# Second block's attention heads: score products alternate between the array's row halves, value products between its column halves

## The chip, the cores and the metric

One core of a Trainium2 chip runs the whole program in one launch. The metric is the device time in microseconds of one execution. The profile is of one further execution, with times relative to the start of its span.

## What is computed

The reference runs two transformer blocks of two layers each over 256 tokens of width 1024, in float32. The change lies in the second block's mixer alone. Each of its two layers projects the normed input to queries, keys and values of heads of width 64, and has three kinds of heads:

```python
def fox_attention(q, k, v, log_f):              # 4 "forget" heads, causal
    s = q k^T / 8 + c_q - c_k                   # c: running sum of the forget gates
def dilated_attention(q, k, v):                 # 4 heads, three dilations, merged by their log sums
def nsa_attention(q, kc, vc, ks, vs, kw, vw, gates, ...):
    # 8 heads in 2 key groups of 4; three branches, mixed by gates:
    # compressed keys; selected blocks (with 4 blocks and top 16, every block); a window of 512 (all keys)
    o = gb[..., 0:1] * o_c + gb[..., 1:2] * o_s + gb[..., 2:3] * o_w
```

Every branch is softmax(scores) times values. The mixer's outputs are projected back by `w_out`, normed and added to the input, and a feed-forward part follows.

## The kernel before, in words

The kernel is written with tile pools, and a planner turns the program into one fixed instruction order for each engine: it goes through the program in order of emission, simulates the time, and issues on each engine the earliest emitted instruction whose inputs and slots are there. Semaphores are set by it.

The 256 tokens are two token tiles of 128. Large products (`mm3`, L220 to L222) take three products of float32r parts each. They write to PSUM tiles `g`, of which there are four, one bank each. Another four banks, `t`, serve transposes and value products.

`attend` (L711) holds the mixer's heads. Projections of column groups 5, 1, 2, 0, 3, 4 (`proj`) stand between them. `heads` (L739) transposes queries and keys, so that head features lie on partitions: an even head, or key group 0, on partitions 0 to 63, an odd head, or key group 1, on 64 to 127. A score product then contracts over 64 partitions and uses half of the array's rows. Queries and keys are float32, so that one product in the code is two passes (two weight loads and two matmuls) in the trace.

- `heads4` (L619) makes a token tile's four dilated ('d') or forget ('f') heads. For each parity of the head a `g` tile gets the mask by a product with an identity (L629, L631), then two score products (L634), all on one row half. Forget heads also get two products of depth 4 with the row of forget sums (L639). A softmax follows (L513: maximum on VectorE, scaling by -1/8 on GpSimd, one exponential per head on ScalarE, reciprocal and scaling on VectorE).
- `nsa_scores` (L654) does the same for one key group `g`, one token tile `t` and one branch `w` (selected or window). At token tile 0 one `g` tile holds all four heads; at token tile 1 two `g` tiles hold two heads each, with 256 keys. L661 is the mask product, L663 the score products.
- The second half of each of these generators transposes the probabilities (L535) and, in `heads4`, multiplies them with the values (L649). Value products have 64 output features, so each uses half of the array's columns.
- `nsa_out` (L694) sums the three branches of both key groups in one `t` tile: group 0 in partitions 0 to 63, group 1 in 64 to 127 (L706).
- `units` (L759) starts each generator, keeps it in a queue, and runs the oldest one's second half when the queue is longer than `DEPTH` = 6.

After `attend`, `wide` (L453) makes the output projection in four `g` tiles. Its first half needs the dilated and forget heads alone.

Of the kernel before, what the change touches and what calls it, by code (L numbers as in the profile page):

```python
# [9 lines left out]
F32 = mybir.dt.float32  # L10
# [19 lines left out]
# which tags of a pool share slots, and the slots' counts  # L30
# [23 lines left out]
class Layout:  # L54
    """Weights as a sequence of [128, 2048] tiles, with the place of each by name."""
# [4 lines left out]
    def add(self, name, w, nk, ncol):  # L60
        """w [K, N] in tiles of nk row blocks by ncol columns; name -> [column group][row group]"""
# [39 lines left out]
def lay_second(inp, l):  # L101
    """The second block's weights and vectors of layer l"""
# [22 lines left out]
def causal_masks():  # L125
    """What the scores of four heads (token tile 0) or two (1) are added to"""
# [6 lines left out]
def constants():  # L133
    """Constants of the shapes alone, each [128, n] float32"""
# [28 lines left out]
DEPTH = 6  # L163


class Core:
# [4 lines left out]
    def tile(self, pool, shape, dt=F32, tag=None, bufs=None):  # L171
        """A tile of a pool: tags of one size share slots, as SHARE has it; BUFS has the slots' counts"""
# [20 lines left out]
    def slot(self):  # L193
        """The pool of the next tile of weights: one in 4 in self.more, if there is any"""
# [3 lines left out]
    def weights(self, src, nk, ncol, pool=None, tag=None, cols=1024):  # L198
        """A tile of weights, nk row blocks by ncol columns: each block as two float32r parts whose sum it is"""
# [17 lines left out]
    def mm3(self, ps, a, b, first, last):  # L217
        """ps += (a0 + a1)^T (b0 + b1) without a1^T b1, which is below float32's last place"""
# [22 lines left out]
    def gemm_t_steps(self, pss, X, tiles, banks=True, tail=1):  # L241
        """The same, step by step: a tile, or of the last ones a token tile"""
# [28 lines left out]
    def rsqrt(self, v, eps, fam, n=1, scale=1.0):  # L271
        """(scale * v + eps) ** -0.5 for a [128, n] tile"""
# [8 lines left out]
    def stats(self, chunks, fam):  # L281
        """mean and variance over the chunks (at most 512 columns each) -> [128, 2]"""
# [10 lines left out]
    def pair(self):  # L293
        """A [128, 8, 256] operand's two parts"""
# [8 lines left out]
    def split(self, shape, src, tag, scale=None, pool=None):  # L303
        """(scale * src) as two float32r parts; src may be in PSUM"""
# [15 lines left out]
class Second(Core):  # L320
    """One layer of the second block, in place on the two token tiles X"""
# [30 lines left out]
    def consts2(self, cm):  # L352
        """Constants of the second block in the types its products take"""
# [10 lines left out]
    def rms_hT(self, X, g, apart=False):  # L364
        """rms_norm(X) * g, transposed: two float32r parts [128, 8, 256]"""
# [1417 lines left out]
```

## Time and profile before

| | us |
|---|---|
| timed runs | 2775.9, 2768.64, 2766.63 |
| median | 2768.64 |
| span of the profiled execution | 2762.7 |
| TensorE busy | 2662.2 (96%) |
| VectorE busy | 1952.3 (71%) |
| ScalarE busy | 1381.0 (50%) |
| 16 DMA engines | 48.6% for weights and rows |

The span runs from the first instruction to the last; the timed runs include what lies around it. Busy times are from the page's first part. The heads of the second block lie at 2058 to 2192 us (first layer) and 2434 to 2553 us (second layer).

### The profile page before, as it was taken

Reading aid. Unit: us, or ns where it says so; the run is one execution under the profiler, and the core shown is the slowest. Engines: PE = TensorE matmul, PEld = TensorE weight load, DVE = VectorE, ACT = ScalarE, POOL = GpSimd, SP = SyncE. Lnnn points to the kernel's source line nnn. Section 1 sums busy time; section 2 is a strip of 40 time slices with the busy share of each in tenths; the row PEclk is TensorE's granted clock in tenths of the full one; section 3 lists DMA queues with packets and bytes.
Section 4 is the critical chain, followed back from the end, with each engine's and each line's share of the span. In section 5 each row is a group of like instructions: output and inputs, shape, how many; then the busy total and the mean of one; then the engine's idle time right before and its main releaser. Section 6 shows DMA issues by size and latency. Waiting matters only on the chain.

```text
span 2762.7 us, 44974 instructions
## 1 busy us (share of the span) xinstructions
PE 2662.2 (96%) x17024; PEld 2276.8 (82%) x17024; DVE 1952.3 (71%) x3898; ACT 1381.0 (50%) x2522; POOL 177.2 (6%) x411
## 2 busy tenths in 40 slices
PE   7999999999999999999999999989989999999999
PEld 5977999977989888887797897979866699776897
DVE  4888977888867633355688997766665589556795
ACT  3555565545555422234754654544554366544563
POOL 0010111000100100001100110010010000000000
PEclk9999999999999999999999999999988799999999
DMA  7566556565536522232555433645644256542454
GB/s 252 185 223 206 169 174 217 171 206 175 171 115 204 170 92 92 94 97 94 170 161 204 150 128 99 201 157 190 191 152 154 70 168 197 169 162 87 152 194 157
DMA packets 127915, 443.31 MB, mean 160 GB/s; under 512 B 14889, under 2 KB 19113, under 8 KB 127697
## 3 DMA queue, kind: packets, MB, share of 16 engines
q1 hardware_dynamic: 127696, 440.43, 48.6%
q8 instruction: 134, 2.20, 0.3%
q14 instruction: 85, 0.69, 0.1%
HBM read 435.09 MB, written 5.28 MB: 159 GB/s over the span
## 4 chain that ended last, share of the span: by engine, by line
PE 47%; DVE 2%; ACT 1%; POOL 1%; issue 1%; DMA 0%; DVEq 0%; POOLq 0%; SPq 0%; ACTq 0%
PE g L221 11%; PE g L220 11%; PE g L222 11%; PE g L663 1%; PE t L221 1%; PE t L222 1%; PE t L220 1%; PE t L535 1%; PE t L706 1%; PE t L1269 1%; PE t L1103 1%; PE t L1140 0%; PE t L1166 0%; PE t L1253 0%; DMA raw<-in_w_dram 0%
## 5 line engine op out<-in xcount | busy, mean ns | idle before, releaser
L213 DVE TENSOR_TENSOR lo<-raw,hi 128x512 fp32r<-128x512 f32 (+2 forms) x1280 | 825.8, 685 | 350.8 <-issue 159.5
L210 ACT CAST hi<-raw 128x1024 fp32r<-128x1024 f32 (+2 forms) x644 | 672.3, 1046 | 726.2 <-PE g L221 249.2
L220 PE MATMUL g<-b,hi 128*128 128x256 f32 (+1 forms) x2912 | 829.8, 287 | 2.2 <-ACT hi L210 1.4
L221 PE MATMUL g<-b,hi 128*128 128x256 f32 (+1 forms) x2912 | 827.5, 286 | 3.2 <-DVE b L314 3.2
L222 PE MATMUL g<-b,lo 128*128 128x256 f32 (+1 forms) x2912 | 821.2, 287 | 2.4 <-DVE lo L213 2.3
L221 PEld LDWEIGHTS g<-b,hi 128*128 128x128 f32 x2912 | 547.4, 188 | 12.9 <-DVE b L314 4.9
L220 PEld LDWEIGHTS g<-b,hi 128*128 128x128 f32 x2912 | 546.9, 188 | 13.5 <-ACT b L313 2.5
L222 PEld LDWEIGHTS g<-b,lo 128*128 128x128 f32 x2912 | 540.6, 188 | 11.9 <-DVE lo L213 3.7
L1281 DVE SCALAR_TENSOR_TENSOR yc<-yc,vec,yc 128x256 f32<-128x256 f32 x720 | 346.3, 481 | 10.8
L221 PE MATMUL g<-lo,b 128*128 128x512 f32 (+2 forms) x712 | 274.8, 386 | 2.9 <-DVE lo L213 2.6
L222 PE MATMUL g<-hi,b 128*128 128x512 f32 (+2 forms) x712 | 266.1, 374 | 0.9 <-DVE b L317 0.8
L220 PE MATMUL g<-hi,b 128*128 128x512 f32 (+2 forms) x712 | 256.2, 378 | 9.5 <-ACT h L522 4.4
L220 PEld LDWEIGHTS g<-hi,b 128*128 128x128 f32 x712 | 135.7, 193 | 38.1 <-ACT h L522 6.8
L221 PEld LDWEIGHTS g<-lo,b 128*128 128x128 f32 x712 | 137.0, 192 | 32.0 <-DVE lo L213 8.4
L222 PEld LDWEIGHTS g<-hi,b 128*128 128x128 f32 x712 | 136.9, 192 | 22.4 <-DVE b L317 1.5
L220 PE MATMUL t<-b,hi 128*128 128x256 f32 (+1 forms) x336 | 111.8, 333 | 0.0
L221 PE MATMUL t<-b,hi 128*128 128x256 f32 (+1 forms) x336 | 111.8, 333 | 0.0
L222 PE MATMUL t<-b,lo 128*128 128x256 f32 (+1 forms) x336 | 111.7, 332 | 0.0
L917 PE MATMUL g<-raw,cs 128*32 128x512 f32 x384 | 84.2, 647 | 14.6 <-DMA raw<-in_w_dram 14.5
L480 DVE SCALAR_TENSOR_TENSOR s<-g,vec,s 128x255 f32<-128x255 f32 (+1 forms) x176 | 84.2, 479 | 6.3 <-ACT s L478 4.1
L220 PEld LDWEIGHTS t<-b,hi 128*128 128x128 f32 x336 | 63.0, 187 | 7.5
L222 PEld LDWEIGHTS t<-b,lo 128*128 128x128 f32 x336 | 63.0, 187 | 7.4
(426 smaller groups left out, 3994.7 us busy)
## 6 DMA issues: line engine op xcount, KB each, us to landing
raw<-in_w_dram SPq DMA_DIRECT2D x772, 512.0 KB
b<-in_row_dram SPq DMA_DIRECT2D x16, 512.0 KB
b<-in_ctx_dram SPq DMA_DIRECT2D x4, 512.0 KB
ends<-st SPq DMA_DIRECT2D x8, 256.0 KB
st<-ends SPq DMA_DIRECT2D x8, 256.0 KB
b<-in_x_dram SPq DMA_DIRECT2D x4, 512.0 KB
b<-ctx SPq DMA_DIRECT2D x4, 512.0 KB
raw<-in_w_dram SPq DMA_DIRECT2D x4, 426.0 KB
```

Of the source, the lines that this page charges most:

```text
L210: self.nc.scalar.copy(hi[:, :m], p)
L213: self.nc.vector.tensor_sub(lo[:, q], p[:, q], hi[:, q].bitcast(F32))
L220: t.matmul(ps, a[0], b[0], start=first, stop=False)
L221: t.matmul(ps, a[0], b[1], start=False, stop=False)
L222: t.matmul(ps, a[1], b[0], start=False, stop=last)
L480: nc.vector.scalar_tensor_tensor(c[:, m, j:], ps[:, m, :256 - j], cw[:, ft, 2 - j:3 - j], c[:, m, j:], op0=ALU.mult, op1=ALU.add)
L535: nc.tensor.transpose(ps[:, i * 128:i * 128 + 128], b, self.ident)
L663: nc.tensor.matmul(ps[:, b], qk['nq', a * per + b][s, t * 128:t * 128 + 128], qk[kn, 0][s, :nk], start=False, stop=b == per - 1)
L706: nc.tensor.matmul(po[s].rearrange("p j q -> p (j q)"), pr[kt][:, col:col + 64], PT_[t, w, g, kt], start=False, stop=w == 1 and kt == t, t ...
L917: nc.tensor.matmul(ps[32 * q:32 * q + 32], self.cs[:, h * 4 + q], raw[:, q % 2 * 512:q % 2 * 512 + 512], start=h == 0, stop=h == 1, tile_p ...
L1103: nc.tensor.matmul(p[:, h], kw[:, d, h * 128:h * 128 + 128], vg[:, h * 256:h * 256 + 256], start=True, stop=True)
L1281: e.scalar_tensor_tensor(o, y[:, j:j + 256], w[:, j:j + 1], o, op0=ALU.mult, op1=ALU.add)
```

## The change

The score products of two PSUM tiles, one for each row half, are now issued in turn. `nsa_scores` makes both key groups in one unit: two mask products, then for each head a product of group 0 and one of group 1, then both softmaxes. In `heads4` the products with the forget sums stand right behind the mask, ahead of the scores. Value products alternate between the column halves from one product to the next. The queue of units is four long instead of six, and the list of units at the end has two score units instead of four. The diff also empties comment lines and docstrings, which are not shown.

```diff
-DEPTH = 6
+DEPTH = 4
...
     def heads4(self, kind, base, t, pr, qk, crow, hi, lo):
-        PS = []
-        for par in range(2):
-            ps = self.tile(self.PG, [128, 512], F32, 'g')[:, :2 * nk].rearrange("p (h k) -> p h k", h=2)
+        pss = [self.tile(self.PG, [128, 512], F32, 'g')[:, :2 * nk].rearrange("p (h k) -> p h k", h=2) for _ in range(2)]
+        for par, ps in enumerate(pss):
             flat = ps.rearrange("p h k -> p (h k)")
             if kind == 'f':
                 cm = self.cmb[t] if t == 1 else self.cmb[0][:, :256]
                 nc.tensor.matmul(flat, self.identb, cm, start=True, stop=False)
+                for b in range(2):
+                    h = 2 * b + par
+                    nc.tensor.matmul(ps[:, b], self.c('self')[:4, h * 128:h * 128 + 128], crow[:, :nk], start=False, stop=False)
             else:
                 nc.tensor.matmul(flat, self.ident, self.c(f'dm{t}'), start=True, stop=False)
-            s = slice(64 * par, 64 * par + 64)
-            for b in range(2):
+        for b in range(2):
+            for par, ps in enumerate(pss):
+                s = slice(64 * par, 64 * par + 64)
                 nc.tensor.matmul(ps[:, b], qk[kind + 'q', b][s, t * 128:t * 128 + 128], qk[kind + 'k', b][s, :nk],
-                                 start=False, stop=kind == 'd' and b == 1)
-            if kind == 'f':
...
-            PS.append(self.softmax(ps, 2, nk))
+                                 start=False, stop=b == 1)
+        PS = [self.softmax(ps, 2, nk) for ps in pss]
...
-        for h in range(4):
-            s = slice(64 * (h % 2), 64 * (h % 2) + 64)
+        for b in range(2):
             for kt in range(t + 1):
...
+                for h in (2 * b, 2 * b + 1):
+                    s = slice(64 * (h % 2), 64 * (h % 2) + 64)
...
-    def nsa_scores(self, t, w, kn, gi, g, pr, qk, ga, PT_):
+    def nsa_scores(self, t, w, kn, gi, pr, qk, ga, PT_):
...
-            ps = self.tile(self.PG, [128, 512], F32, 'g').rearrange("p (h k) -> p h k", h=per)
-            nc.tensor.matmul(ps.rearrange("p h k -> p (h k)"), self.identb, self.cmb[t], start=True, stop=False)
+            pss = [self.tile(self.PG, [128, 512], F32, 'g').rearrange("p (h k) -> p h k", h=per) for _ in range(2)]
+            for ps in pss:
+                nc.tensor.matmul(ps.rearrange("p h k -> p (h k)"), self.identb, self.cmb[t], start=True, stop=False)
             for b in range(per):
-                nc.tensor.matmul(ps[:, b], qk['nq', a * per + b][s, t * 128:t * 128 + 128], qk[kn, 0][s, :nk],
-                                 start=False, stop=b == per - 1)
+                for g, ps in enumerate(pss):
+                    s = slice(64 * g, 64 * g + 64)
+                    nc.tensor.matmul(ps[:, b], qk['nq', a * per + b][s, t * 128:t * 128 + 128], qk[kn, 0][s, :nk],
+                                     start=False, stop=b == per - 1)
...
     def nsa_out(self, t, pr, cmp, PT_, hi, lo):
-        for g in range(2):
-            s = slice(64 * g, 64 * g + 64)
-            for w, vn in enumerate(('vs', 'vw')):
-                for kt in range(t + 1):
-                    col = P2[vn] + 64 * g
+        for w, vn in enumerate(('vs', 'vw')):
+            for kt in range(t + 1):
+                for g in range(2):
+                    s, col = slice(64 * g, 64 * g + 64), P2[vn] + 64 * g
...
-        units(scores(0, 0, 0), scores(0, 0, 1))
+        units(scores(0, 0))
...
-        units(scores(0, 1, 0), scores(0, 1, 1))
+        units(scores(0, 1))
...
-        units(four('f', 2, 0), scores(1, 0, 0))
+        units(four('f', 2, 0))
         next(cv, None)
-        units(four('f', 2, 1), scores(1, 0, 1), self.nsa_compressed(0, qk, cmp, ga, PT_), scores(1, 1, 0),
-              self.nsa_out(0, pr, cmp, PT_, hi, lo), self.nsa_compressed(1, qk, cmp, ga, PT_), scores(1, 1, 1),
+        units(four('f', 2, 1), scores(1, 0), self.nsa_compressed(0, qk, cmp, ga, PT_),
+              self.nsa_out(0, pr, cmp, PT_, hi, lo), scores(1, 1), self.nsa_compressed(1, qk, cmp, ga, PT_),
               self.nsa_out(1, pr, cmp, PT_, hi, lo))
```

## Rows read from the trace of the kernel before

**Rows 1.** The page's first part: engine, busy us, share, instructions.
```profile
PE 2662.2 (96%) x17024; PEld 2276.8 (82%) x17024; DVE 1952.3 (71%) x3898; ACT 1381.0 (50%) x2522; POOL 177.2 (6%) x411
...
```

**Rows 2.** Busy time in the stretches around the heads; columns in the first line.
```profile
core 0: us, PE busy (x) PEld busy (x) DVE busy (x) ACT busy (x) POOL busy (x), PEclk, DMA share, GB/s
2092.90:2100.60 7.70, 7.49 (x72) 5.28 (x71) 3.26 (x11) 5.38 (x20) 0.69 (x3) 1.00 0.48 153
2115.60:2161.80 46.20, 46.20 (x193) 30.11 (x192) 26.48 (x87) 16.90 (x54) 5.09 (x11) 0.61 0.20 70
...
2488.50:2524.30 35.80, 35.80 (x192) 24.17 (x191) 22.77 (x75) 15.31 (x49) 3.71 (x9) 0.81 0.28 89
2524.30:2552.90 28.60, 28.09 (x156) 18.58 (x155) 18.42 (x43) 13.35 (x31) 1.27 (x3) 1.00 0.23 73
```

**Rows 3.** The same view, cut where the granted clock changes.
```profile
2119.05:2129.28 10.23, 10.23 (x45) 6.13 (x47) 5.43 (x19) 2.69 (x10) 1.24 (x3) 0.50 0.01 2
...
2136.12:2166.80 30.68, 30.68 (x101) 21.59 (x100) 15.61 (x56) 8.22 (x29) 2.75 (x6) 0.50 0.12 39
...
2504.80:2518.40 13.60, 13.60 (x56) 10.07 (x55) 6.67 (x23) 3.82 (x12) 1.14 (x2) 0.50 0.29 95
```

**Rows 4.** Timeline of TensorE, token tile 0; start us, us, instruction, shapes, count.
```profile
2093.01 1.71 PE L663 MATMUL g<-h,h 64*128 64x128 f32 x16
...
2096.95 0.39 PE L661 MATMUL g<-cmb,identb 128*128 128x512 bf16 x1
2097.27 1.16 PE L663 MATMUL g<-h,h 64*128 64x128 f32 x8
2098.36 0.39 PE L661 MATMUL g<-cmb,identb 128*128 128x512 bf16 x1
...
2099.76 0.63 PE L581 MATMUL t<-cst,s 128*128 128x32 f32 x4
```

**Rows 5.** Timeline of ScalarE after token tile 0's scores.
```profile
2101.33 1.05 ACT L210 CAST hi<-raw 128x1024 fp32r<-128x1024 f32 x1 [0.74 <-DMA raw<-in_w_dram]
```

**Rows 6.** Timeline of TensorE, forget heads of token tile 1, first layer.
```profile
2133.45 1.13 PE L634 MATMUL g<-h,h 64*128 64x256 f32 x4
2134.51 1.13 PE L639 MATMUL g<-s,cst 4*128 4x256 f32 x4
```

**Rows 7.** Timeline of TensorE, scores of token tile 1 in both layers.
```profile
2156.65 0.63 PE L661 MATMUL g<-cmb,identb 128*128 128x512 bf16 x1
...
2159.22 0.61 PE L661 MATMUL g<-cmb,identb 128*128 128x512 bf16 x1
...
2521.56 0.38 PE L661 MATMUL g<-cmb,identb 128*128 128x512 bf16 x1
2521.87 1.13 PE L663 MATMUL g<-h,h 64*128 64x256 f32 x4
2522.93 0.39 PE L661 MATMUL g<-cmb,identb 128*128 128x512 bf16 x1
```

**Rows 8.** Timeline of TensorE, value products of both token tiles, first layer.
```profile
2181.97 1.94 PE L706 MATMUL t<-h,proj 128*64 128x512 f32 x8
2183.85 0.33 PE L535 MATMUL t<-cst,s 128*128 128x128 f32 x1
...
2186.11 4.56 PE L706 MATMUL t<-h,proj 128*64 128x512 f32 x14
2190.60 0.49 PE L220 MATMUL g<-h,b 128*128 128x512 f32 x1
2191.03 1.07 PE L706 MATMUL t<-h,proj 128*64 128x512 f32 x2
2192.03 0.49 PE L221 MATMUL g<-h,b 128*128 128x512 f32 x1
```

**Rows 9.** Softmax groups by line, both layers; a wait of TensorE, first layer.
```profile
L517 DVE TENSOR_REDUCE s_a<-g 128x2 f32<-128x512 f32 x24 | 16.2, 675 | 1.6 <-PE g L639 1.6
...
L518 POOL TENSOR_SCALAR s_a<-s_a 128x2 f32<-128x2 f32 x32 | 13.7, 429 | 202.8 <-DVE s_a L517 150.6 <-DVE s_a L526 36.0 <-DVE gx L586 7.1
...
L522 ACT ACTIVATE h<-g,s_a 128x256 f32<-128x256 f32 x48 | 22.3, 472 | 27.8 <-POOL s_a L518 27.8
...
PE g L220 <- ACT h L522: 2.0, 1, 2.0
```

More of the change, by code (lines that the diff above doesn't have):

```diff
@@ L645, in heads4 @@
         col = P2[kind + 'v']
-        for h in range(4):
-            s = slice(64 * (h % 2), 64 * (h % 2) + 64)
+        for b in range(2):
             for kt in range(t + 1):
-                nc.tensor.matmul(po[s, h // 2], pr[kt][:, col + 64 * h:col + 64 * h + 64], pts[kt][:, h * 128:h * 128 + 128],
-                                 start=kt == 0, stop=kt == t, tile_position=(0, 64 * (h % 2)))
+                for h in (2 * b, 2 * b + 1):
+                    s = slice(64 * (h % 2), 64 * (h % 2) + 64)
+                    nc.tensor.matmul(po[s, b], pr[kt][:, col + 64 * h:col + 64 * h + 64], pts[kt][:, h * 128:h * 128 + 128],
+                                     start=kt == 0, stop=kt == t, tile_position=(0, 64 * (h % 2)))
@@ L651, in heads4 @@
         ts = slice(t * 128, t * 128 + 128)
         self.split_to(hi[:, base:base + 2, ts], lo[:, base:base + 2, ts], po)
[L654 removed]
+    def nsa_scores(self, t, w, kn, gi, pr, qk, ga, PT_):
         nc = self.nc
[L657 to L658 removed]
+        nk, per = 128 * (t + 1), 4 // (t + 1)
+        Ps = [[], []]
         for a in range(t + 1):
[L660 to L661 removed]
+            pss = [self.tile(self.PG, [128, 512], F32, 'g').rearrange("p (h k) -> p h k", h=per) for _ in range(2)]
+            for ps in pss:
+                nc.tensor.matmul(ps.rearrange("p h k -> p (h k)"), self.identb, self.cmb[t], start=True, stop=False)
@@ L662, in nsa_scores @@
             for b in range(per):
-                nc.tensor.matmul(ps[:, b], qk['nq', a * per + b][s, t * 128:t * 128 + 128], qk[kn, 0][s, :nk],
-                                 start=False, stop=b == per - 1)
-            h0 = 4 * g + a * per
-            Ps.append(self.softmax(ps, per, nk, ga[:, t, h0:h0 + per, gi]))
+                for g, ps in enumerate(pss):
+                    s = slice(64 * g, 64 * g + 64)
+                    nc.tensor.matmul(ps[:, b], qk['nq', a * per + b][s, t * 128:t * 128 + 128], qk[kn, 0][s, :nk],
+                                     start=False, stop=b == per - 1)
@@ L667, in nsa_scores @@
+            for g, ps in enumerate(pss):
+                h0 = 4 * g + a * per
+                Ps[g].append(self.softmax(ps, per, nk, ga[:, t, h0:h0 + per, gi]))
         yield
-        for kt in range(t + 1):
-            PT_[t, w, g, kt] = self.transposed([Ps[j // per][:, j % per, kt * 128:kt * 128 + 128] for j in range(4)])
+        for g in range(2):
+            for kt in range(t + 1):
+                PT_[t, w, g, kt] = self.transposed([Ps[g][j // per][:, j % per, kt * 128:kt * 128 + 128] for j in range(4)])
@@ L700, in nsa_out @@
                              start=j == 0, stop=False)
-        for g in range(2):
-            s = slice(64 * g, 64 * g + 64)
-            for w, vn in enumerate(('vs', 'vw')):
-                for kt in range(t + 1):
-                    col = P2[vn] + 64 * g
+        for w, vn in enumerate(('vs', 'vw')):
+            for kt in range(t + 1):
+                for g in range(2):
+                    s, col = slice(64 * g, 64 * g + 64), P2[vn] + 64 * g
                     nc.tensor.matmul(po[s].rearrange("p j q -> p (j q)"), pr[kt][:, col:col + 64], PT_[t, w, g, kt],
@@ L764, in units @@
                     next(queue.pop(0), None)
-        scores = lambda t, w, g: self.nsa_scores(t, w, ('ks', 'kw')[w], w + 1, g, pr, qk, ga, PT_)
+        scores = lambda t, w: self.nsa_scores(t, w, ('ks', 'kw')[w], w + 1, pr, qk, ga, PT_)
         four = lambda kind, base, t: self.heads4(kind, base, t, pr, qk, crow, hi, lo)
```

6 lines of the change are left out of this document (removed).

## The prediction

> **What bounds the kernel now.** The page's table of busy times comes first. TensorE is busy for 2662.2 of 2762.7 us and VectorE, the next engine, for 71% of the span [rows 1]. So time is won where TensorE's work becomes shorter, as long as nothing that hid behind it comes forward. The change touches only the second block's heads, which run once in each of its two layers, so the next view is the table of stretches around them [rows 2]. Four stretches matter. "A" holds the scores of token tile 0 (2092.9 to 2100.6 us in the first layer). "B0" (2115.6 to 2161.8) and "B1" (2488.5 to 2524.3) hold the forget heads and the scores of token tile 1 of the first and the second layer. "C" (2524.3 to 2552.9 in the second layer) holds transposes, value products and the first half of the output projection. The reader is to see three things there. TensorE is busy for all of B0 and B1, so nothing else sets their length. VectorE has 22.77 us of work in the 35.8 us of B1. And B0 takes 10.4 us longer than B1 for the same instructions (193 and 192 records), at a mean granted clock of 0.61 instead of 0.81. The third view, the same table cut where the clock changes, shows TensorE at the lower of its two levels (1.2 instead of 2.4 GHz) for 10.2 and 30.7 us in the first layer and 13.6 us in the second [rows 3].
>
> The last view is the timeline of TensorE. Each float32 product is issued as two passes, so the timeline counts two for every product in the code.
>
> **The change part by part.** (1) Scores, token tile 0, selected keys. Eight passes of one key group (the upper 64 rows of the array) and then eight of the other (the lower 64 rows) lasted 1.71 us, while eight alone lasted 1.16 [rows 4]. If all sixteen went one after another they would need about twice the spacing of an eight, 2 x 1.09 (2097.27 to 2098.36). So products on different row halves do run side by side on this chip, and even issued group after group they overlap in part. In strict alternation they would take what eight take: 1.71 - 1.16 = 0.55 us saved.
>
> The Trainium skill, page "TensorE: Matmul & The Clock Gate", section "Part 3: Packing small matmuls — row/col tiling", says that products on different tiles of the array run concurrently, and also that products start and end strictly in issue order. By the second half of that rule nothing would overlap when a whole group is issued before the other, and alternation would save 2 x 1.09 - 1.16 = 1.0 us here instead of 0.55. The row of the sixteen passes speaks against it, so I go by the row.
>
> (2) Scores, token tile 0, window keys. Now a mask product (L661) stands in front of each group, and the two blocks take 2096.95 to 2099.76 = 2.81 us [rows 4]. Afterwards there are two mask products, 0.32 each by the first one's spacing, and one alternated run of 1.09: 1.73. Saved 1.1 us.
>
> (1) and (2) make 1.65 us per layer, but what follows is the projection of column group 4, whose second weight tile is cast only at 2101.33, when its DMA has landed [rows 5]. TensorE would come earlier and wait there. The bounds are 0 and 1.65 us; I take 0.5, because the weights' landing is moved only as far as their slots come free earlier. Two layers: 1.0.
>
> (3) Forget heads. The four score products of a token tile now go together, and the four products with the row of forget sums (4 rows deep, all on the same rows) move ahead of them, unpaired as before. What goes is one of two score runs: 1.06 us at token tile 1 (2133.45 to 2134.51) [rows 6], and about half of an eight, 0.55, at token tile 0. Saved 1.6 per layer. The moved products need only the forget sums and the constants; nothing new is waited for.
>
> (4) Scores, token tile 1: eight blocks per layer, each a mask product and four passes on one row half. At full clock a block takes 2521.56 to 2522.93 = 1.37 us, of which the mask is 0.31 and the scores 1.06; at the lower clock 2156.65 to 2159.22 = 2.57 us [rows 7]. Afterwards there are four pairs of 2 x 0.31 + 1.06 = 1.68 us at full clock. Saved 8 x 1.37 - 4 x 1.68 = 4.2 us.
>
> (3) and (4) make 5.8 us per layer at full clock. In B0 a mean clock of 0.61 means that 0.39/0.5 = 78% of the stretch, and so 0.39/0.61 = 64% of its work, went at the lower level; at 2.57/1.37 = 1.88 times the price that makes 5.8 x (0.36 + 0.64 x 1.88) = 9.1 us. Together 14.9 us. How much reaches the end depends on VectorE, ScalarE and GpSimd, which make the softmax between the scores and the transposes. B1 would hold 22.77 us of VectorE work in 30 us, so there is room, but VectorE works in a fixed order and waits for TensorE inside it. From both sides: all of it, since TensorE waits for nothing in B0 and B1 today, or a fifth (3 us), if the softmaxes become the limit. I take 60%, 9.0 us.
>
> (5) Value products. At token tile 0 of the compressed, selected and window branches (L706), two runs of four passes, one after another in the code, already lie side by side: 2181.97 to 2183.85 = 1.88 us for eight passes. At token tile 1 two runs of eight passes take 2186.11 to 2192.03 = 5.92 us with one projection product inside, 0.43 (2190.60 to 2191.03) [rows 8]. Alternated, sixteen passes take at most twice the 1.88: 3.76. Saved 5.92 - 0.43 - 3.76 = 1.7 per layer. The forget and dilated heads' value products alternate already at token tile 0 and are counted at nothing: their cover is the overlap that the row of token tile 0 shows, and without it the gain would only be larger. Two layers give 3.4 at most, 0 if the last transposes come late; I take 3.0.
>
> (6) The queue of units. Its limit goes from six to four, and a unit of scores is now both groups; before, the six held single groups. The transposes are the same in number and come from the queue two groups at a time. I cost this at nothing, since the projection's products fill TensorE between them in C; without that cover a late group of transposes costs one softmax chain, about 3.7 us by the rival below. No DMA is added, removed or reissued; the weight loads only follow the slots that TensorE frees.
>
> (7) The clock. The lower level came in B0 and B1 after stretches in which single runs on half the rows, or on four rows, filled TensorE, and it stayed through the unpaired scores until transposes and projections came. Paired runs work on twice the rows at once. Whether that keeps the clock up no row shows. The bounds are the 10.4 us that B0 lost against B1 gained in the first layer, or the same lost in the second. I take a quarter of it as gain, 2.6.
>
> Sum: 1.0 + 9.0 + 3.0 + 2.6 = 15.6 us. The profiled execution's span is 2762.7; the median of the three timed runs is 2768.64, so 5.9 us lie around the span if that execution was a median one. Forecast: span 2747, time 2753 us.
>
> **The rivals.** *The whole gain and the clock.* All of the bounds above: 3.3 + 14.9 + 3.4 + 10.4 = 32.0, time 2737. For it speaks that TensorE waits nowhere in B0 and B1; against it that three other engines would have to be early everywhere.
>
> *Softmax keeps the pace.* A pair needs two of the four PSUM banks. Until both are free again after its scores there are two maxima (0.675 each), one scaling on GpSimd (0.43) and four exponentials (0.47 each): 3.7 us [rows 9]. The old order needs one bank at a time and hides this behind longer score runs. If that takes back four fifths of (3) and (4) and all of (5), the clock stays as it is, and 1.0 + 3.0 = 4 us remain: 2765. The Trainium skill, page "TensorEngine Tiling (Array Packing)", section "PSUM Bottleneck", states this in general: packing speeds up TensorE but not the emptying of PSUM. The trace agrees in so far as TensorE does wait for exponentials once today, 2.0 us before the projection of group 0 [rows 9]; in B no wait is seen.
>
> *The order isn't kept.* Instructions are issued by a planner that takes what is ready, so pairs may be torn apart by transposes or by the second query tile. Then nothing of (3) and (4) remains and half of (5), under 2 us: 2767.
>
> *Slower.* If between pairs there is nothing else to issue, each of the six pairs per layer (two of forget heads, four of scores) waits 3.7 - 1.68 = 2.0 us for its banks, 12 x 2.0 = 24 us. TensorE then idles, and B1 loses the clock as B0 did: 10.4 more. Against 15.6 us of savings (11.6 of (3) and (4) at full clock, 3.0, 1.0) that is 18.8 us slower: 2787. It decides from a mean wait of 15.6/12 = 1.3 us per pair on. Against it: compress, transposes and value products lie between the score blocks today.
>
> **How the numbers follow.** About 0.3% (8.3 us) is what can be told from no change, so faster means under 2760.3 and slower over 2777. Forecast (2741 to 2762): 0.54. Whole gain and clock: 0.13. Softmax pace: 0.18. Order not kept: 0.06. Slower: 0.09. Nearly all of the forecast and the first rival is faster: 0.65. The rest of the forecast and the two middle rivals make 0.26. The range 2736 to 2769 takes in the first rival's time and most of the middle ones.
>
> **What would show it.** Right: in the timeline, score runs of token tile 1 as eight passes in some 1.1 us at full clock behind two mask products, and value runs of sixteen passes in under 4 us. B1 should shrink to about 32 us, B0 to 37 to 40, and C by 1 to 2 us. The softmax rival would show as idle time of TensorE before mask products, released by ScalarE's exponentials (L522); the weights' limit as a longer wait for ScalarE's cast in A. The prediction is wrong if B0 and B1 keep their lengths with TensorE idle in them, or if the lower clock lasts longer than the 54.5 us of today.

## The result, and the profile after

The changed kernel takes 2739.49 us, the median of four runs (2735.17 to 2745.55); beside it the kernel before took 2767.64 (four runs, 2763.62 to 2775.9). The ratio is 0.9888, 95% interval 0.9859 to 0.9917. (The ratios given here are not the quotients of the medians; the two differ by up to 0.0013.) Measured once more beside the last group of experiments, it was 2751.37 us (12 runs) against 2769.93: 0.9942, 0.9920 to 0.9965. So the change is faster both times, by 19 to 28 us; the two intervals just miss each other.

The forecast was 2753 us, in a range that holds both times. That it came so near is luck, since its working doesn't hold: TensorE's work shrank by a few microseconds where the sum had 13, and most of the gain is TensorE running less at its lower clock, a term that the sum had at 2.6 us.

The first part of the page after. TensorE's busy time is 25.4 us less than before [rows 1], with the same 17024 matmuls. The page of the profiled execution gives a span of 2743.8 us, and that execution took 2745.55: 1.75 us lie around the span, not the 5.9 of the prediction (whose span of 2747 us is thus a time of 2749).

```profile
span 2743.8 us, 44955 instructions
...
PE 2636.8 (96%) x17024; PEld 2259.1 (82%) x17024; DVE 1950.9 (71%) x3898; ACT 1381.8 (50%) x2522; POOL 172.8 (6%) x411
```

The stretches A (first layer), B0, C of the first layer, B1 and C of the second, in the view of rows 2:

```profile
core 0: us, PE busy (x) PEld busy (x) DVE busy (x) ACT busy (x) POOL busy (x), PEclk, DMA share, GB/s
2097.20:2104.90 7.70, 7.48 (x74) 4.97 (x73) 3.08 (x8) 4.79 (x17) 0.46 (x2) 1.00 0.54 169
2118.90:2152.20 33.30, 29.86 (x200) 19.46 (x199) 24.43 (x77) 16.70 (x53) 3.31 (x10) 0.95 0.29 97
2152.20:2176.80 24.60, 23.97 (x138) 16.85 (x138) 15.92 (x40) 10.87 (x25) 0.48 (x2) 1.00 0.21 66
2476.30:2511.00 34.70, 31.56 (x201) 19.96 (x199) 24.37 (x77) 16.92 (x54) 3.31 (x10) 0.90 0.28 92
2511.00:2535.70 24.70, 24.02 (x139) 16.89 (x139) 16.01 (x40) 10.87 (x25) 0.48 (x2) 1.00 0.20 64
```

Three things are to be seen. The granted clock in B0 is 0.95 where it was 0.61, in B1 0.90 where it was 0.81 [rows 2]. TensorE now has some 3 us without work in each B, where it had none. And the second C is 24.7 us where it was 28.6. Cut where the clock changes, two low pieces are left in B, 3.4 and 6.8 us, in place of 10.2, 30.7 and 13.6 [rows 3]:

```profile
2126.60:2130.00 3.40, 3.40 (x26) 1.61 (x20) 1.29 (x2) 2.16 (x3) 0.00 (x0) 0.50 0.80 264
2481.60:2488.40 6.80, 6.80 (x29) 2.90 (x27) 1.88 (x4) 2.81 (x6) 0.00 (x0) 0.50 0.57 176
```

TensorE's timeline tells which products really alternate (lines moved: 663 is now 667, 661 is 662, 634 is 638, 639 is 631, 706 is 711). The selected pair of token tile 0 does: sixteen passes in 1.16 us where they took 1.71 [rows 4]. Its window pair is torn by the second mask:

```profile
2097.30 1.16 PE L667 MATMUL g<-h,h 64*128 64x128 f32 x16
...
2101.01 1.16 PE L667 MATMUL g<-h,h 64*128 64x128 f32 x8
2102.09 0.39 PE L662 MATMUL g<-cmb,identb 128*128 128x512 bf16 x1
2102.41 1.16 PE L667 MATMUL g<-h,h 64*128 64x128 f32 x8
```

The forget heads do alternate. At token tile 1 the four products stand as two pairs with value products between them. Each pair, four passes, takes 1.16 us at the lower clock (2487.28 to 2488.44) and 0.63 at full clock (2489.03 to 2489.66), where four unpaired passes took 1.06 [rows 6]. In the second layer, shown here, the lower clock came during the four-row sums ahead of them, which therefore last 1.72 and 2.07 us:

```profile
2479.90 1.07 PE L575 MATMUL g<-raw,s 128*32 128x256 f32 x16 [1.68 <-issue]
...
2481.22 1.72 PE L631 MATMUL g<-s,cst 4*128 4x256 f32 x4
...
2483.41 2.07 PE L631 MATMUL g<-s,cst 4*128 4x256 f32 x4
...
2487.28 1.23 PE L638 MATMUL g<-h,h 64*128 64x256 f32 x4
2488.44 0.66 PE L649 MATMUL t<-h,proj 128*64 128x128 f32 x8
2489.03 0.70 PE L638 MATMUL g<-h,h 64*128 64x256 f32 x4
2489.66 0.39 PE L662 MATMUL g<-cmb,identb 128*128 128x512 bf16 x1
```

The selected and window scores of token tile 1 are as before, mask and one group, mask and the other group, 1.37 us a block [rows 7]:

```profile
2142.35 0.38 PE L662 MATMUL g<-cmb,identb 128*128 128x512 bf16 x1
2142.66 1.13 PE L667 MATMUL g<-h,h 64*128 64x256 f32 x4
2143.72 0.39 PE L662 MATMUL g<-cmb,identb 128*128 128x512 bf16 x1
```

The value products of token tile 1 alternate: sixteen passes in 3.65 us, where they took 5.92 with one projection product of 0.43 inside [rows 8]:

```profile
2173.24 3.65 PE L711 MATMUL t<-h,proj 128*64 128x512 f32 x16
```

TensorE's waits from 2062 to 2200 us (engine, tile and line that waited, releaser: us in total, times, longest). The wait for an exponential before the projection was 2.0 [rows 9]; the three others in the stretch of the heads are new:

```profile
PE g L220 <- ACT h L522: 2.4, 2, 2.1
PE g L575 <- issue: 1.7, 1, 1.7
...
PE t L649 <- DVE s_b L695: 0.9, 1, 0.9
PE t L705 <- DVE h L542: 0.6, 1, 0.6
```

Between the two profiled executions B0 and B1 together lost 13.6 us (45.9 + 35.6 to 33.3 + 34.6, from the first score product to the first projection product), both C 9.6 (58.8 to 49.2), and everything else gave 4.3 us back. Some 2.5 of these 4.3 are work that only changed places: the sums of token tile 0 stood behind the first scores and now stand ahead of them, four times 0.63 us that B no longer holds. Low clock in B fell from 49.6 to 10.2 us; at the 1.88 of the prediction's steps (3) and (4), 39.4 us less of it are worth 39.4 x (1 - 1/1.88) = 18.4 us. Another 5.0 us of it lay in the first C of the kernel before, until 2166.80 [rows 3], and is gone too: 2.3 of C's 9.6 us, at the same price.

### The profile page after: what moved, and what is told of

Read it like the earlier page. It is cut to its first block, busy times and chain, and to the rows that moved or that the text cites. A ratio compares the mean times of both kernels' runs of the same rounds, so it can differ in the third digit from the quotient of the medians.

```text
span 2743.8 us, 44955 instructions
## 1 busy us (share of the span) xinstructions
PE 2636.8 (96%) x17024; PEld 2259.1 (82%) x17024; DVE 1950.9 (71%) x3898; ACT 1381.8 (50%) x2522; POOL 172.8 (6%) x411
## 4 chain that ended last, share of the span: by engine, by line
PE 87%; DVE 3%; DMA 3%; ACT 2%; POOL 2%; issue 2%; SPq 0%; DVEq 0%; POOLq 0%; ACTq 0%
PE g L221 20%; PE g L220 20%; PE g L222 20%; PE t L220 3%; PE t L222 3%; PE t L221 3%; DMA raw<-in_w_dram 3%; PE g L922 2%; PE t L1145 2%; PE t L1171 1%; PE t L1274 1%; PE t L1258 1%; PE t L1108 1%; PE t L1180 1%; DVE lo L213 1%
## 5 line engine op out<-in xcount | busy, mean ns | idle before, releaser
L221 PEld LDWEIGHTS g<-lo,b 128*128 128x128 f32 x712 | 137.0, 192 | 31.5 <-DVE lo L213 7.4
```

Source lines behind the costliest of these rows:

```text
L221: t.matmul(ps, a[0], b[1], start=False, stop=False)
```

## The experiments

Two theories stood at the start: the gain is TensorE work (pairs, value products), or it is the granted clock, kept up by one part of the change; the expectations of the first four kernels call the ways in which the clock could do it 1, 1a and 1b. The kernels of a group of four ran on one chip beside the kernel before, the three groups on three chips. "Clock" is the mean granted clock over the runs. The last two columns are the lengths of B0 and B1 in the profiled execution, from the forget heads' first score product to the first projection product behind the last scores, with the low clock in them (where the sums go ahead of the scores, token tile 0's two groups of them, 0.6 us each, lie before that start, in the changed kernel from 2110.92 and from 2118.30 us; such a B holds 1.3 us less work).

| kernel | median us (runs) | ratio, 95% interval | clock | B0 (low) | B1 (low) |
|---|---|---|---|---|---|
| before, first group | 2772.89 (23) | | 0.973 | 45.9 (35.9) | 35.6 (13.7) |
| e1_value | 2775.70 (12) | 1.0007 [0.9982, 1.0032] | 0.971 | 35.6 (13.7) | 35.6 (13.7) |
| e2_forget | 2755.60 (6) | 0.9937 [0.9915, 0.9959] | 0.978 | 35.5 (17.1) | 28.2 (0) |
| e3_units | 2768.11 (12) | 0.9991 [0.9973, 1.0010] | 0.975 | 46.8 (27.3) | 46.5 (27.3) |
| e5_pairs | 2744.05 (4) | 0.9902 [0.9877, 0.9927] | 0.980 | 33.8 (13.7) | 33.3 (6.8) |
| before, second group | 2770.98 (17) | | 0.972 | | |
| f1_sums | 2748.84 (6) | 0.9924 [0.9907, 0.9941] | 0.981 | 30.9 (6.8) | 30.9 (6.8) |
| f2_rows | 2760.07 (12) | 0.9961 [0.9946, 0.9976] | 0.975 | 36.4 (17.1) | 42.0 (29.2) |
| f3_deep | 2745.75 (6) | 0.9908 [0.9891, 0.9924] | 0.983 | 29.2 (0) | 29.7 (0) |
| f4_both | 2756.36 (6) | 0.9945 [0.9926, 0.9965] | 0.976 | 35.3 (17.1) | 35.3 (17.1) |
| before, third group | 2769.93 (30) | | 0.973 | | |
| g3_control | 2764.97 (12) | 0.9995 [0.9972, 1.0019] | 0.974 | 46.0 (36.1) | 35.6 (13.7) |
| g1_afterdeep | 2749.70 (9) | 0.9938 [0.9915, 0.9962] | 0.980 | 35.9 (6.8) | 36.4 (6.8) |
| g2_bothdeep | 2748.70 (10) | 0.9920 [0.9896, 0.9944] | 0.980 | 37.5 (18.2) | 29.4 (3.4) |
| g4_after | 2751.37 (12) | 0.9942 [0.9920, 0.9965] | 0.978 | 32.8 (3.4) | 47.3 (32.4) |

**One part at a time.** e1_value is the kernel before with the alternating value products alone:

```diff
-        for g in range(2):
-            s = slice(64 * g, 64 * g + 64)
-            for w, vn in enumerate(('vs', 'vw')):
-                for kt in range(t + 1):
-                    col = P2[vn] + 64 * g
+        for w, vn in enumerate(('vs', 'vw')):
+            for kt in range(t + 1):
+                for g in range(2):
+                    s, col = slice(64 * g, 64 * g + 64), P2[vn] + 64 * g
```

> The kernel before with the value products alone alternating between the column halves (in the heads' second half and in the sum of the three branches). Theory 1 (the clock made most of the gain, and the scores' new order made the clock): 3 to 5 us faster, only stretch C shorter (value run of token tile 1 from 5.92 to under 4 us), B0 still at a mean clock near 0.61 and 46 us long. Rival (the value products carry the gain): 10 us or more faster.

No difference in time. The run of value products did shrink, 14 of 16 passes from 4.56 [rows 8] to 3.65 us:

```profile
2167.52 3.65 PE L706 MATMUL t<-h,proj 128*64 128x512 f32 x14
```

Its 12 runs are spread over 43 us, from 2745.89 at a clock of 0.980 to 2788.53 at 0.965. So a microsecond or two of work per layer is there and can't be seen under the clock. (Its profile is of its fastest run, so its B0 is not typical.)

e2_forget is the kernel before with the new order of the dilated and forget heads alone: sums behind the mask, scores on the row halves in turn, both softmaxes after.

```diff
-        for par in range(2):
...
+        for b in range(2):
+            for par, ps in enumerate(pss):
+                s = slice(64 * par, 64 * par + 64)
                 nc.tensor.matmul(ps[:, b], qk[kind + 'q', b][s, t * 128:t * 128 + 128], qk[kind + 'k', b][s, :nk],
...
```

> The kernel before with the new order of the forget and dilated heads' score products alone (forget sums ahead, row halves in turn). Theory 1a (the clock stays up in B because the forget heads no longer run alone on few rows): B0 at a mean clock over 0.8 and under 40 us, 10 to 15 us faster. Theory 1b (the units' new order, with transposes between score blocks, keeps the clock): 0 to 3 us faster, B0 still over 43 us.

More than half of the change's first ratio comes with this part, and the clock with it.

e3_units is the kernel before with the merged selected and window units, the new list and the shorter queue (`DEPTH = 4`); forget heads and values as before.

> The kernel before with both key groups in one unit, the new list of units and a queue of four; forget heads and value products as before. Theory 1a: 0 to 5 us faster, B0 still over 43 us at a clock under 0.7. Theory 1b: B0 under 40 us, 10 to 15 us faster. Rival (the gain is a run's chance in the clock, tied to neither part): times as the kernel before within 5 us, with clocks that differ from run to run.

Nothing in the time. Both B are some 47 us long, with 27.3 us of low clock. The score pairs are torn here too (blocks of a mask and four passes), and B0 already has three of the waits of the changed kernel, 1.7 us before L575, 0.9 before L649 and 0.3 for an exponential, which neither f1_sums nor f4_both below, with the old units, has there. So those waits come with the new units and the shorter queue; which of the two was not separated.

e5_pairs is the changed kernel, with the score products held back until both masks are issued, so that all pairs alternate:

```diff
+                    with self.tc.issue_after(mask.ins):
                         nc.tensor.matmul(ps[:, b], qk['nq', a * per + b][s, t * 128:t * 128 + 128], qk[kn, 0][s, :nk],
...
```

> The changed kernel, with the score products of a pair held back until both mask products are issued, so that the pairs of the eight heads' scores are not torn apart by the planner. If the torn order is why step (4) of the prediction brought nothing (blocks of 4 passes in 1.13 us after a mask each): 8 passes in about 1.2 us, B1 3 to 5 us shorter than the changed kernel's 35.4, time 5 to 10 us under the changed kernel's 2739. If banks and softmax bind: the same time as the changed kernel within 3 us, with TensorE idle before mask products, released by exponentials.

The pairs are real: eight passes in 1.14 us behind two masks, where four took 1.13.

```profile
2498.96 0.38 PE L662 MATMUL g<-cmb,identb 128*128 128x512 bf16 x1
2499.26 1.14 PE L668 MATMUL g<-h,h 64*128 64x256 f32 x8
2500.33 0.89 PE L662 MATMUL g<-cmb,identb 128*128 128x512 bf16 x2
2501.16 1.14 PE L668 MATMUL g<-h,h 64*128 64x256 f32 x8
```

And they bring nothing clear in the time: 0.9902 lies between the changed kernel's 0.9888 and 0.9942, and its interval overlaps both. In B1 TensorE is busy for 27.5 of 33.3 us (31.6 of 34.7 in the changed kernel): of 4.1 us less work, 2.7 are spent waiting. In B0 it waits 3.4 us, as in the changed kernel, but has 13.7 us of low clock in place of 3.4. Reckoned at full clock with the price of 1.88, an estimate, B0 and B1 are 27.4 and 30.1 us, in the changed kernel 31.7 and 31.5. So the pairs do free time in B, and the clock and the waits take it back. The sign that the expectation names, idle time before mask products until an exponential, is only 0.7 us in B0 and 0.3 in B1; the longer waits (1.3 to 1.7 us each) are for VectorE and before L575.

**What in the forget heads' order holds the clock.** Three theories, which have nothing to do with the stretches of the same letters: theory A, the sums' new place; theory B, the row halves in turn; theory C, the products over 4 rows, which the sums are.

By their edits, f1_sums has the sums behind the mask and nothing else (the diff), and f2_rows has the row halves in turn and nothing else, the edit of e2_forget with the sums left behind the scores.

```diff
                 nc.tensor.matmul(flat, self.identb, cm, start=True, stop=False)
+                for b in range(2):
+                    h = 2 * b + par
+                    nc.tensor.matmul(ps[:, b], self.c('self')[:4, h * 128:h * 128 + 128], crow[:, :nk],
+                                     start=False, stop=False)
...
-            if kind == 'f':
-                for b in range(2):
```

> The kernel before, with one edit: for both token tiles of the forget heads the four-row sum products are issued right behind the mask product, ahead of the score products; the score products stay half after half, the softmax of the first pair of heads stays where it was, the value products too. The run with the whole new order of the forget and dilated heads gave 0.9937 of the kernel before (2755.6 us, mean granted clock 0.978 against 0.973). Theory A (the place of the sums carries that: they are ready earlier and run among other work): about 2756 us, ratio 0.992 to 0.996, clock 0.977 or more. Theory B (single score products on one half of the array's rows drag the clock, and pairing them is what helps): ratio 0.998 to 1.003, clock 0.972 to 0.974, about 2771. Theory C (products over four rows drag the clock, wherever they stand): no gain here either, 0.998 to 1.003, since there are as many of them.

> The kernel before, with one edit: in the forget and dilated heads both masks are issued first and the score products then on the two row halves in turn; the four-row sums stay behind the scores, and the value products are as before. Theory A (place of the sums): ratio 0.997 to 1.002, clock as before. Theory B (row halves in turn): it carries the whole gain of the new order of these heads, 2753 to 2758 us, ratio 0.992 to 0.996, clock 0.977 or more. Theory C (four-row products): about 0.998 to 1.002. In the trace the eight passes of the dilated heads should run side by side (about 0.7 us per pair of heads against some 1.1) under every theory; what differs is the clock.

f1 gains as theory A had it (0.9924). f2 gains half of that (0.9961), more than A and less than B expected. Theory C as it was put, four-row products "wherever they stand", is out: f1 has as many of them.

The traces show that the two edits don't part A from B as they were meant to. In f1_sums nothing stands between the scores of the two row halves at token tile 0 any more, and they run side by side, eight passes in 0.65 us (2119.41 to 2120.06), though the code has one half after the other. In f2_rows token tile 0 has the same, but at token tile 1 the planner issues the four passes of one half and its sums before the second mask, as in the kernel before; no pair is formed there. First f1_sums, then f2_rows:

```profile
2119.41 0.72 PE L638 MATMUL g<-h,h 64*128 64x128 f32 x8
```

```profile
2123.96 1.13 PE L635 MATMUL g<-h,h 64*128 64x256 f32 x4
2125.02 1.13 PE L641 MATMUL g<-s,cst 4*128 4x256 f32 x4
2126.08 0.39 PE L628 MATMUL g<-cmb,identb 128*128 128x512 bf16 x1
2126.40 1.13 PE L635 MATMUL g<-h,h 64*128 64x256 f32 x4
```

So both kernels have the pairs of token tile 0 and none at token tile 1, and what f1_sums has over f2_rows, on the same chip and with intervals that don't meet, is in the main the place of the sums. e2_forget, where one of the two pairs of token tile 1 is formed (four passes in 0.70 us in the second layer), gains no more than f1_sums.

f3_deep leaves the order alone and makes the sum products 128 rows deep:

```diff
-        crow = self.tile(self.P, [128, 256], F32, 's1')[:4]
-        nc.vector.tensor_scalar(crow, pc, -8.0, None, op0=ALU.mult)
+        crow = self.tile(self.P, [128, 256], F32, 's1')
+        nc.vector.memset(crow, 0.0)
+        nc.vector.tensor_scalar(crow[:4], pc, -8.0, None, op0=ALU.mult)
...
-                    nc.tensor.matmul(ps[:, b], self.c('self')[:4, h * 128:h * 128 + 128], crow[:, :nk],
+                    nc.tensor.matmul(ps[:, b], self.c('self')[:, h * 128:h * 128 + 128], crow[:, :nk],
```

> The kernel before, with one edit: the forget heads' sum products run over all 128 rows of the array (the factor's other 124 rows are zeros) in place of 4; their number, length and place stay. The result is the same; one more memset of 128x256 per layer is added on the vector engine. Theory C (products over four rows drag the clock): mean clock 0.978 or more, 2750 to 2757 us, ratio 0.992 to 0.996, and less low clock in the stretch of the second block's heads. Theories A and B: ratio 0.998 to 1.003, clock 0.972 to 0.974, about 2771.

g3_control has the same tile and the same memset, and the sums still over 4 rows (`self.c('self')[:4, h * 128:h * 128 + 128]` with `crow[:4, :nk]`). TensorE's instructions stand in the same order as in f3_deep, from first to last.

> The kernel before, with the same memset of 128x256 per layer as in the run with the deep sums, and the tile kept at 128 rows, but the forget heads' sum products still over 4 rows. The run with the sums over 128 rows gave 0.9908 of the kernel before (2745.8 us, clock 0.983). Theory C (depth of the sum products decides the clock): no gain here, ratio 0.998 to 1.003, clock 0.971 to 0.975, low clock again in the stretch of the forget and selected heads. Rival (any small shift of what is issued when moves the clock, and the depth has nothing to do with it): the same gain as with the deep sums, ratio 0.989 to 0.993, clock 0.98 or more.

In the old order the depth of the sum products decides, as theory C has it. f3_deep gives 0.9908, more than expected; the control, on another chip and beside the kernel before as well, gives nothing. B0 and B1 of f3_deep, then of the control, the same instructions in each:

```profile
2114.30:2143.50 29.20, 28.97 (x192) 19.58 (x191) 22.25 (x74) 15.06 (x48) 3.67 (x9) 1.00 0.32 111
2469.70:2499.40 29.70, 29.04 (x192) 19.52 (x191) 22.56 (x74) 15.17 (x49) 3.69 (x9) 1.00 0.33 107
```

```profile
2118.50:2164.50 46.00, 45.75 (x191) 30.17 (x191) 26.36 (x86) 16.90 (x54) 4.34 (x10) 0.61 0.20 71
2491.50:2527.20 35.70, 35.45 (x192) 24.08 (x191) 22.74 (x74) 15.30 (x49) 3.69 (x9) 0.81 0.28 89
```

The sum products themselves last as long over 4 rows as over 128 (x32 in the span; ns, least, median, most): first f3_deep, then the control.

```profile
L639 PE MATMUL g<-s,cst x32: 275/378/483, 2115.2 to 2484.2; 128*128 128x128 f32 x16, 128*128 128x256 f32 x16
```

```profile
L639 PE MATMUL g<-s,cst x32: 270/373/478, 2119.4 to 2506.3; 4*128 4x128 f32 x16, 4*128 4x256 f32 x16
```

What differs is what follows them. Behind the forget heads of token tile 1 in f3_deep, at full clock throughout:

```profile
2128.29 1.13 PE L639 MATMUL g<-s,cst 128*128 128x256 f32 x4
2129.26 0.38 PE L661 MATMUL g<-cmb,identb 128*128 128x512 bf16 x1
2129.57 1.13 PE L663 MATMUL g<-h,h 64*128 64x256 f32 x4
2130.62 1.14 PE L649 MATMUL t<-h,proj 128*64 128x128 f32 x16
```

and in the control, where the same four scores take 1.99 us and the value products 2.03, because the clock goes to its lower level (1.2 of 2.4 GHz) right there and stays for 30.7 us:

```profile
2137.40 1.12 PE L639 MATMUL g<-s,cst 4*128 4x256 f32 x4
2138.46 0.39 PE L661 MATMUL g<-cmb,identb 128*128 128x512 bf16 x1
2138.78 1.99 PE L663 MATMUL g<-h,h 64*128 64x256 f32 x4
2140.70 2.03 PE L649 MATMUL t<-h,proj 128*64 128x128 f32 x16
```

**Does it add up?** f4_both is the kernel before with the new forget and dilated order and the alternating values together; g2_bothdeep the same with deep sums; g1_afterdeep the changed kernel with deep sums; g4_after the changed kernel itself.

> The kernel before with two parts of the change together and without the third: the new order of the forget and dilated heads and the value products on alternating column halves; the selected and window scores, their list of units and the depth stay as before. The work at full clock should be the lowest of all runs under every theory, about 2689 us (2696 less 2.2 and 4.9). If the parts' effects on the clock simply add (0.978 of the one, 0.971 of the other), the clock is 0.976 to 0.978 and the time 2748 to 2755. If it is the three parts together that keep the clock (theory: the merged units' place in the order does it), the clock stays at 0.974 and the time is 2758 to 2765. If the heads' order and the value products are all that matters in the change, it is as fast as the whole change, 2735 to 2745, ratio 0.988 to 0.991, clock 0.981.

The clock is the 0.976 of the first case, in which the parts' effects add, and the time, 2756.36, lies 1.4 us over its range. It is far from the 2735 to 2745 of the last case; but these came from the first measurement of the whole change. Beside the second (0.9942) the two parts' 0.9945 is as much as the whole.

> The changed kernel with the forget heads' sum products over all 128 rows. Theory C: the low clock that is left in the stretch of the forget and selected heads (3.4 us in the first layer, 6.8 in the second) goes, which is worth about half of it, 5 us; the time is 2733 to 2739, ratio to the kernel before 0.986 to 0.989, clock 0.984. Rival (the change's own gain in clock has another source than the four-row products): the two gains add, 0.980 to 0.984. If the new place of the sums had already taken all that there is to take: as the changed kernel, 2738 to 2745.

> The kernel before with the new order of the forget and dilated heads, the alternating value products, and the sums over all 128 rows; selected and window scores, units and depth as before. Without the deep sums this gave 2756.4 us (0.9945, clock 0.976, 34 us of low clock in the two stretches of the forget and selected heads, 2691 us at full clock). Theory C: that low clock goes, worth some 17 us, 2735 to 2741, ratio 0.986 to 0.990, clock 0.983. Rival (the low clock comes from the selected and window scores on half of the rows, which stay as they were): 2750 to 2757, clock 0.977.

> The changed kernel once more, unedited, beside the others on the same chip, for the comparison with the deep sums: 2735 to 2746 us, ratio 0.986 to 0.992, clock 0.980 to 0.985. If its clock were an accident of its first four runs: 2745 to 2760.

g4_after took 2751.37 us at a clock of 0.978, where the first four runs had 0.982: its expectation's second case, so part of the first 0.9888 was a lucky clock. And here theory C finds its end. In the changed kernel deep sums add nothing (0.9938 beside 0.9942). g2_bothdeep, at 2748.70 between its two expectations, still has 18.2 us of low clock in B0, with no product over 4 rows left. g4_after, whose profiled execution took 2762.92 us, shows where low clock can still come from: B1 at a granted clock of 0.66, 47.3 us long.

```profile
2477.90:2525.20 47.30, 42.67 (x200) 28.40 (x199) 24.12 (x75) 16.40 (x53) 3.30 (x10) 0.66 0.21 68
```

```profile
2494.39 0.38 PE L662 MATMUL g<-cmb,identb 128*128 128x512 bf16 x1 [1.60 <-ACT h L522]
2494.70 1.13 PE L667 MATMUL g<-h,h 64*128 64x256 f32 x4
2496.31 0.69 PE L611 MATMUL t<-s1b,s 128*128 128x64 f32 x2 [0.49 <-DVE s L608]
2496.80 1.92 PE L535 MATMUL t<-cst,h 128*128 128x128 f32 x8
```

Ahead of this fall lie scores on half of the rows and two waits, 1.60 us for an exponential and 0.49 for VectorE. Two like them, 1.23 and 1.07 us, stand ahead of the fall in g2_bothdeep. In g1_afterdeep TensorE, at full clock until then, waits before a mask for an exponential in both layers, 2.47 us (until 2127.61) and 3.05 (until 2486.00); its only low clock in B, 6.8 us in each layer, begins near the end of these waits. The first one in its table of waits:

```profile
PE g L662 <- ACT h L522: 2.5, 1, 2.5
```

With the others it makes 5.4 us of waits in B0, where the changed kernel has 3.4. That the waits bring the clock down is only argued: no run took them away with all else kept, and in e5_pairs a wait of 1.54 us for VectorE (before 2490.92) passes without a fall. The kernel that would join the old order, deep sums and alternating values was not run, and f3_deep and the changed kernel were never on the same chip, so none of the experiments is shown to beat the changed kernel.

## Why the prediction was right in its number and wrong in its working

That the forecast of 2753 us came so near is luck: step (4) was much too high, step (7) much too low, and the two errors nearly cancel. The first time, 2739.49, lies below the 2741 to 2762 that the prediction gave its forecast and next to the rival "whole gain and clock" (2737), whose mechanism didn't hold either; the second, 2751.37, lies inside.

**Steps (1) and (2)**, 1.0 us: the 0.55 of the selected pair came as worked out; the 1.1 of the window pair didn't, since the pair is torn. In the second layer TensorE then waits 1.3 us for the cast of the projection's weights, as the step had foreseen, and meets 3.4 us of low clock; from these scores to B it is 1.3 us less in the first layer and 3.2 more in the second. Nothing in sum is to be seen; but this stretch has also taken in the 1.3 us of sums, and in the first layer it has lost 3.4 us of low clock (2102.0 to 2105.4 in the kernel before).

**Step (3)**, the forget heads, came nearly as worked out: at token tile 1 two runs of 1.06 became two of 0.63, and at token tile 0 eight passes take 0.65 us (2118.93 to 2119.58) where g3_control needs 2 x 0.64; 1.5 us of work per layer against 1.6. At token tile 0 the alternation itself is not what does it: in f1_sums the same eight passes take 0.65 us with one half after the other in the code, once the sums are out from between them.

**Step (4)**, the larger part of the 9.0 us, is the step that failed, and what held in its place is the mechanism of the rival "the order isn't kept", to which I gave 0.06: four passes in 1.06 us behind each mask, where the prediction's sign of being right was eight behind two. The planner issues whatever is ready; by that rule the first group's scores were ready before the second group's mask was, so the pairs of token tile 1 stay single. The step was wrong in its overlap too: with the order forced in e5_pairs the scores cost what the step says, but in B1 2.7 of the 4.1 us freed go into waits, and in B0 the lower clock takes the gain back.

At full clock B even became longer: 33.3 us with 3.4 low and 34.7 with 6.8 make 31.7 and 31.5 at the price of 1.88, against the 29.2 and 29.7 of f3_deep in the old order. **Step (6)**, costed at nothing, is the reason as far as the traces tell: some 3 us without work in each B. Three of the waits, 2.9 us together, stand in B0 of e3_units as well, which has the new units and the queue of four alone, and not in f1_sums or f4_both, which have the old ones. Another part is work moved up from C, which is shorter by 4.0 us in the second layer, more than the value products gave.

**Step (5)**, 3.0 us, is right in its work: 5.92 - 0.43 - 3.65 = 1.84 per layer, against 1.7. In the time of e1_value nothing of it can be seen.

**Step (7)**, the clock, 2.6 us: the term that was mis-sized. Its lower level in B fell by 39.4 us in the profiled executions, worth 18.4. Over all runs, time times mean granted clock, a rough figure for the time at full clock, is 2694 to 2696 us before and 2691 to 2693 after; so of the mean difference (some 15 us in the second measurement, 28 or more in the first) 1 to 5 us are work. (By the same figure f3_deep is at 2699: none of its gain is work.) The prediction did say what the engine did before the fall (runs on half of the rows, or on four) and kept the 10.4 us between B0 and B1 as a bound; it took that bound for the whole of what the clock could cost. f3_deep shows it: 16.8 us in B0 and 5.9 in B1.

The mechanism was half wrong too. It is not the pairing of the selected and window scores that holds the clock: in the changed kernel those of token tile 1 are not paired, and e3_units kept the lower clock. It is the forget heads' new order. Taking the four-row sums from between the half-row score runs is most of it: f1_sums, whose edit is only that, comes to 0.9924, between the two measurements of the whole change. f2_rows, which forms the pairs of token tile 0 and leaves the sums behind the scores, gives 0.9961, and with a pair of token tile 1 as well as the sums' new place the gain is no greater (e2_forget, 0.9937). Why the place of the sums matters, when their depth alone also decides, no run shows.

The Trainium skill, page "TensorE: Matmul & The Clock Gate", section "HAM oscillation — how this bites in real kernels", puts such a fall down to gaps in which TensorE has nothing to do. In B0 and B1 of the kernel before there is no such gap (46.20 busy of 46.20 us [rows 2]), and yet the clock fell; f3_deep and its control show products over few rows doing it with TensorE busy in all but 0.25 us of each B of the control. The waits ahead of the falls in g4_after, g2_bothdeep and g1_afterdeep are gaps too, but e5_pairs has one without a fall.

## What to carry to other kernels

When a stretch shows a granted clock below 1.00 with TensorE busy in all of it, look for products over few rows in it, and try the same product over all 128 rows with zeros: its own time hardly changes, and in the old order 32 such passes of 17024 decided 20 to 24 us (f3_deep against its control, by medians or by ratios). It is no rule: in the changed kernel the same edit brought nothing. Before counting on an interleaved order of products, see that the planner can keep it: here whatever is ready is issued, so a pair needs both of its masks first; and see in the timeline of each experiment that the order meant is the order issued. And time a change of a few microseconds by its stretches in the profile, since a kernel's runs differ by more than that through the clock alone.

## What was not expected of the hardware

- Depth 4 or 128 makes no difference to a product's own time (median 373 and 378 ns), but one of 16.8 us to B0 around it, through the clock.
- The runs of one unchanged kernel differ by the granted clock: over the 30 runs of the kernel before in the third group, a line through time and mean clock falls by 2.5 us for each 0.001 of clock (0.970 to 0.979; 2752.57 to 2778.76 us).
- Score passes on the two row halves run side by side also where the code has one half after the other, if nothing stands between them: eight in 0.65 us in f1_sums, as in the alternated order of the changed kernel, and 2 x 0.64 with the sums in between (g3_control).
- Sixteen value passes that alternate between the column halves take 3.65 us, two thirds of the 5.49 that they take in two runs.
